# A hybrid recurrent and attention layer on one core: the second half of the program issued in stated order

## The chip, the cores and the metric

The kernel runs on one core of a Trainium2 chip. The core has a matrix engine (PE, with its weight loads shown apart as PEld), a vector engine (DVE), a scalar engine (ACT), GpSimd (POOL) and a sync engine (SP). In this kernel SP and POOL issue all DMA transfers; POOL issues nearly all stores of the second half, SP nearly all loads. The metric is the device time of one execution in microseconds, the median of several runs.

## The reference

The reference is one inference step of one layer, for a prompt of 2048 frames and a running stream of 64 frames, all in float32:

```python
xn = rmsnorm(x, norm_mix)
x_rnn, y_gate, q, k, v, g_rnn, g_attn = split(xn @ w_in)          # 1024 -> 5632
xc = causal_dwconv(x_rnn, width 4);  h = rg_lru(xc)               # linear recurrence
y_rnn  = h * gelu(y_gate)
y_attn = banded attention of 16 heads over 4 key groups, with rotary q, k and a sink logit
mixed  = sigmoid(g_rnn) * y_rnn + sigmoid(g_attn) * y_attn
x = x + mixed @ w_out                                              # 1024 -> 1024
up = rmsnorm(x, norm_ffn) @ w_up                                   # 1024 -> 5632
gate, val = split(causal_dwconv(up, width 3))
x = x + (silu(gate) * val) @ w_down                                # 2816 -> 1024
y = rmsnorm(x, norm_final)
```

Besides `y` it returns the new attention caches, the recurrent state and the convolution states.

## The kernel before

The frames of both streams stand side by side, 2112 columns, with channels on the 128 partitions. Every float32 product is made of three products in a reduced float32 format: an operand is split into a high part (`hi`, an ACT copy, line 198) and a low part (`lo = src - hi`, mostly on DVE, line 199), and `hi*hi`, `hi*lo` and `lo*hi` are added up in PSUM. So each operand that reaches PE has passed ACT and then DVE.

**First half.** Input projection, recurrence and attention, in three column blocks, up to `es1.close()` at line 719. The last thing that it leaves behind is the tensor `mixS` in DRAM.

**Output projection** (`wout`, `residual`, `mixes`, `wload`, `wsplit`, the loop from line 1258). The columns are taken in three pairs of blocks: phase 0 and phase 1 with two blocks of 304 columns, phase 2 with two of 448. In each phase a loop over `m` (8 row tiles of the output) calls `rows` (POOL loads of `x`), `wout` (48 matmuls over two half tiles of weights `j = 2m, 2m + 1`), `residual` (DVE adds, POOL stores to `x1S`, squares on ACT) and `drive(side, ...)`, which runs some steps of a side job. In phase 0 the weights come raw from DRAM (`wload`, line 375, two buffers), are split (`wsplit`) and their halves are stored to `woS` for the later phases, which load them from there (line 378). The side job of phase 0 is `mixes(1)` and `mixes(2)`: it loads `mixS` for the two later phases (line 358) and splits it, five steps behind each `m`. It has two buffers from line 1262 on, and the text of one step is a split followed by the load that takes over the buffer just split:

```python
        for j, (k, t0, n) in enumerate(todo):
            split(xblocks[t0][:, k, 0], xblocks[t0][:, k, 1], raw[j])
            load()
            yield
```

The side job of phases 1 and 2 is `xprep` (lines 773 to 815): it loads `x1S`, normalizes it (DVE, line 788), forms sums and differences and splits them into operands of the up projection.

**Up projection** (loop from line 1316). It is a fast matrix product with seven products in place of eight for each 2 by 2 block, so a group of weight rows takes seven steps `u = 0..6`. In steps 0 to 139 of the plan two lanes (two pairs of column blocks) share a group's weights; steps 140 to 167 have one lane each; the last 77 have two lanes on the third pair. One step states, in this order: work put off from earlier steps (`later`, filled by `at(d, f)`: convolution, gate, sums, stores), the products on PE (lines 1038 to 1040, 12 matmuls a lane), `prepare(i + ahead)` (the weights of a later step: for four of the seven steps a sum or difference on DVE at line 905, then `hi`, then `lo`; in later groups a load of the stored halves at line 901), `after(u)` (ACT copies of PSUM at line 1085, DVE sums at lines 1089, 1091 and 1096, ACT convolution term at line 1068), and then background jobs: `drive(x1, 5)` in the first four steps, `drive(fill, 1)` from step 6 on (`xsums`, lines 951 to 986, and `wsums`, lines 919 to 949, which prepare operands of the third pair), `xread` in the steps with one lane and the first of the third pair.

**Down projection** (loop over `seq`, line 1444 on). The same fast product in seven parts over 11 tiles; the weights are drawn from DRAM and combined (`draws`), the tokens loaded from `hS` (line 1207) and split (`parts`), with the final residual (`resid`, line 1422), squares and norm as side jobs.

What sets the order: tile buffers in this half are parts of a few large regions, handed out in the order of the text. The framework follows which instruction needs which other through them, and it decides the order in which each engine and each DMA queue gets its instructions: it takes the earliest in the text that a timing model says is ready, so instructions whose inputs the model expects late are passed by others. The order is fixed when the program is built; on the chip each engine runs its list from the front, and an instruction waits on semaphores for what it needs.

Of the kernel before, what the change touches and what calls it, by code (L numbers as in the profile page):

```python
# [126 lines left out]
def kernel(ctx: ExitStack, tc: tile.TileContext, xT, w_in, w_out, w_up, w_dn, gw, pk,  # L127
# [591 lines left out]
    es1.close()  # L719


    es2 = ExitStack()
    pff = es2.enter_context(tc.tile_pool(name="pff", bufs=5, space=PSUM))
    bank = [0]

# [926 lines left out]
```

## Time and profile before

| what | value |
|---|---|
| median of 3 runs | 3017.7 us (3002.41, 3018.79, 3017.7) |
| the profiled execution's own time | 3009.77 us |
| its span (first to last instruction) | 3008.0 us |
| mean granted clock of PE | 0.982 |
| matmuls | 17640 |

The profile was taken of one execution. Its page gives busy times, shares and the costliest groups of instructions; views of the trace give the same for any stretch of the span, group instructions by line, list them in order of time, or sum who waited for whom. In the view of windows each row is a stretch in us from the span's start, then the busy time of each engine with its number of instructions, the granted PE clock (1.00 is full), the busy share of the DMA engines and what they moved. The output projection begins at about 1366 us, the up projection at 1582 us, the down projection at 2530 us. Matmuls overlap, so the distance between their starts, not their duration, says how fast they follow each other.

### The profile page before, as it was taken

The page shows a single profiled execution, that of the slowest core. Times are in us where ns is not written, and L with a number is a line of the kernel's source. Part 1 is how long each engine was busy: PE and PEld are TensorE (multiplying, and loading weights), DVE is VectorE, ACT ScalarE, POOL GpSimd, SP SyncE. Part 2 cuts the span into 40 slices and gives each one's busy share as a digit, 9 for nine tenths or more (in the row PEclk, how much of TensorE's full clock was granted, in tenths as well). Part 3 has the DMA queues.
Part 4 walks back from the last instruction along what each step waited for, and adds up shares of the span by engine and source line. Part 5 has one row for each costly group of instructions (what it writes and reads, how often), then busy time and mean ns, then how long its engine had stood idle before and what let it go on. Part 6 is the DMA issues. An engine that isn't in the chain of part 4 may idle for free.

```text
span 3008.0 us, 49081 instructions
## 1 busy us (share of the span) xinstructions
PE 2877.2 (96%) x17640; PEld 2763.7 (92%) x17640; DVE 2052.4 (68%) x4048; ACT 1557.2 (52%) x3426; POOL 449.1 (15%) x655
## 2 busy tenths in 40 slices
PE   8999999999999999998999999999899999899998
PEld 7989888999998999997898999999899999799998
DVE  5288784377775277775669888777666657566766
ACT  4577772466763367764325445554544445334442
POOL 3232112000000000002222333222111111000001
PEclk9999999999999999999999999999999999999999
DMA  6766547543335643438776666555876667976653
GB/s 238 272 223 202 177 147 239 188 138 125 122 123 173 198 139 127 130 104 302 257 249 221 240 213 219 195 193 199 282 237 214 218 225 220 279 216 197 204 149 123
DMA packets 324501, 595.38 MB, mean 198 GB/s; under 512 B 37168, under 2 KB 224544, under 8 KB 307360
## 3 DMA queue, kind: packets, MB, share of 16 engines
q1 hardware_dynamic: 285728, 461.45, 48.6%
q0 software_dynamic: 38528, 130.79, 11.7%
q8 instruction: 139, 2.28, 0.3%
q14 instruction: 106, 0.87, 0.1%
HBM read 400.99 MB, written 191.64 MB: 197 GB/s over the span
## 4 chain that ended last, share of the span: by engine, by line
PE 68%; DVE 11%; DMA 8%; issue 7%; ACT 3%; POOL 2%; SPq 1%; DVEq 0%; POOLq 0%; ACTq 0%
PE mm L224 9%; PE mm L225 9%; PE mm L223 8%; PE mf L1038 4%; PE mf L1040 4%; PE mf L1039 4%; PE mf L1469 3%; PE mf L1470 3%; PE mf L1468 3%; PE mm L1038 3%; PE mm L1040 2%; PE mm L1039 2%; DMA FW<-mixS 2%; PE mm L1469 1%; PE mm L1470 1%
## 5 line engine op out<-in xcount | busy, mean ns | idle before, releaser
L223 PE MATMUL mm<-xh,whl 128*128 128x320 f32 (+2 forms) x2112 | 690.8, 327 | 11.3 <-ACT xh L198 5.9
L224 PE MATMUL mm<-xl,whl 128*128 128x320 f32 (+2 forms) x2112 | 689.2, 326 | 6.5 <-DVE xl L199 3.7
L225 PE MATMUL mm<-xh,whl 128*128 128x320 f32 (+2 forms) x2112 | 686.6, 325 | 1.4 <-POOL whl L199 1.4
L198 ACT ACTIVATE RE<-FW 128x512 fp32r<-128x512 f32 (+2 forms) x540 | 295.3, 559 | 384.4 <-PE mm L1470 59.2
L223 PEld LDWEIGHTS mm<-xh,whl 128*128 128x128 f32 x2112 | 401.4, 190 | 19.4 <-ACT xh L198 9.1
L224 PEld LDWEIGHTS mm<-xl,whl 128*128 128x128 f32 x2112 | 401.8, 190 | 15.9 <-DVE xl L199 6.5
L225 PEld LDWEIGHTS mm<-xh,whl 128*128 128x128 f32 x2112 | 402.2, 190 | 2.3 <-POOL whl L199 1.7
L199 DVE TENSOR_TENSOR RE<-FW,RE 128x512 fp32r<-128x512 f32 (+2 forms) x540 | 316.3, 600 | 127.1 <-ACT RE L198 125.6
L1038 PE MATMUL mf<-RA,RE 128*128 128x304 f32 (+1 forms) x608 | 200.4, 330 | 0.5 <-DVE FA L1089 0.5
L1040 PE MATMUL mf<-RA,RE 128*128 128x304 f32 (+1 forms) x608 | 199.7, 328 | 0.0
L1039 PE MATMUL mf<-RA,RE 128*128 128x304 f32 (+1 forms) x608 | 199.4, 328 | 0.0
L1469 PE MATMUL mf<-RE 128*128 128x304 f32 (+2 forms) x616 | 197.3, 320 | 0.6 <-DVE RE L199 0.6
L1468 PE MATMUL mf<-RE 128*128 128x304 f32 (+2 forms) x616 | 196.8, 320 | 0.0
L1470 PE MATMUL mf<-RE 128*128 128x304 f32 (+2 forms) x616 | 196.2, 319 | 0.0
L1038 PE MATMUL mf<-RE 128*128 128x304 f32 (+1 forms) x488 | 160.6, 329 | 12.6 <-ACT FA L1085 6.3
L1074 DVE SCALAR_TENSOR_TENSOR FW<-FA,pkt,FW 128x608 f32<-128x608 f32 x176 | 147.6, 844 | 18.3 <-ACT FW L1068 18.0
L1040 PE MATMUL mf<-RE 128*128 128x304 f32 (+1 forms) x488 | 159.9, 328 | 0.2 <-DVE RE L199 0.2
L1039 PE MATMUL mf<-RE 128*128 128x304 f32 (+1 forms) x488 | 159.6, 327 | 0.0
L199 POOL TENSOR_TENSOR gl<-gr,gh 128x256 fp32r<-128x256 f32 x24 | 22.3, 929 | 786.4 <-ACT gh L198 786.4
L1038 PE MATMUL mm<-RE 128*128 128x304 f32 (+1 forms) x392 | 126.5, 323 | 10.8 <-ACT FA L1085 7.6
L496 ACT ACTIVATE pr<-S,nm 128x256 f32<-128x256 f32 (+1 forms) x272 | 122.7, 464 | 12.6 <-DVE nm L492 12.4
L1040 PE MATMUL mm<-RE 128*128 128x304 f32 (+1 forms) x392 | 126.7, 323 | 2.7 <-DVE RE L199 2.7
(339 smaller groups left out, 7253.9 us busy)
## 6 DMA issues: line engine op xcount, KB each, us to landing
whl<-wiS SPq DMA_DIRECT2D x88, 1024.0 KB, 5.1
RE<-wuS SPq DMA_DIRECT2D x104, 512.0 KB, 4.4
wiS<-whl SPq DMA_DIRECT2D x44, 1024.0 KB, 4.8
wuS<-RE POOLq DMA_DIRECT2D x80, 512.0 KB, 4.1
FW<-in_w_up_dram SPq DMA_DIRECT2D x158, 256.0 KB, 3.5
hS<-FA POOLq DMA_DIRECT2D x154, 152.0 KB, 4.0
FW<-hS SPq DMA_DIRECT2D x154, 152.0 KB, 3.3
wraw<-in_w_in_dram SPq DMA_DIRECT2D x44, 512.0 KB, 5.8
```

What stands on the lines that cost most here:

```text
L198: nc.scalar.activation(hi, src, AF.Copy)
L199: (lo_eng or nc.vector).tensor_tensor(lo, src, hi.bitcast(F32), op=ALU.subtract)
L223: nc.tensor.matmul(ps[:, :n], wh[:, c], xh[:, k, :n], start=first, stop=False)
L224: nc.tensor.matmul(ps[:, :n], wh[:, c], xl[:, k, :n], start=False, stop=False)
L225: nc.tensor.matmul(ps[:, :n], wl[:, c], xh[:, k, :n], start=False, stop=last)
L1038: nc.tensor.matmul(ps[:, :n], w[:, 0, c], x[:, k, 0], start=first, stop=False, **more)
L1039: nc.tensor.matmul(ps[:, :n], w[:, 0, c], x[:, k, 1], start=False, stop=False, **more)
L1040: nc.tensor.matmul(ps[:, :n], w[:, 1, c], x[:, k, 0], start=False, stop=last, **more)
L1074: nc.vector.scalar_tensor_tensor(uc, G[:, j:j + self.cols], col("fw", 44 * j + m), uc, op0=ALU.mult, op1=ALU.add)
L1468: nc.tensor.matmul(ps[m][:, cs], w[:, 0, c], t[:, 0], start=k == 0, stop=False)
L1469: nc.tensor.matmul(ps[m][:, cs], w[:, 0, c], t[:, 1], start=False, stop=False)
L1470: nc.tensor.matmul(ps[m][:, cs], w[:, 1, c], t[:, 0], start=False, stop=k == 10)
```

## The change

The second half of the kernel is put under a scope in which every engine and every DMA queue takes its instructions in the order in which the text states them. No instruction, buffer or shape is changed; only the order in which each engine's and each queue's list is written. The scope holds to the end of the program, as `es2` is closed by its last line.

```diff
@@ -719,7 +719,9 @@
     es1.close()
 
 
+
     es2 = ExitStack()
+    es2.enter_context(tc.manual_schedule())
     pff = es2.enter_context(tc.tile_pool(name="pff", bufs=5, space=PSUM))
     bank = [0]
```

## The prediction

> **What bounds the kernel now.** The page's busy times say that PE works in nearly the whole span of 3008.0 us, and the view of windows says where it does not.
>
> ```profile
> PE 2877.2 (96%) x17640; PEld 2763.7 (92%) x17640; DVE 2052.4 (68%) x4048; ACT 1557.2 (52%) x3426; POOL 449.1 (15%) x655
> ```
>
> ```profile
> 1366.00:1441.00 75.00, 63.61 (x389) 58.76 (x388) 37.90 (x81) 29.78 (x64) 27.42 (x46) 0.90 0.96 339
> 1441.00:1505.00 64.00, 59.33 (x394) 57.69 (x393) 41.98 (x90) 24.45 (x52) 14.96 (x28) 0.95 0.79 253
> 1505.00:1582.00 77.00, 77.00 (x380) 71.16 (x379) 51.04 (x103) 21.47 (x45) 20.14 (x37) 1.00 0.75 249
> 1582.00:1890.00 308.00, 287.39 (x1964) 282.73 (x1963) 260.63 (x481) 152.88 (x364) 108.00 (x198) 0.97 0.65 225
> 1890.00:2090.00 200.00, 199.36 (x1410) 199.36 (x1411) 156.98 (x260) 106.02 (x246) 47.87 (x89) 0.98 0.54 186
> 2090.00:2160.00 70.00, 56.97 (x351) 54.02 (x351) 46.39 (x79) 35.64 (x79) 10.19 (x19) 0.90 0.82 271
> 2160.00:2560.00 400.00, 400.00 (x2042) 372.65 (x2041) 255.00 (x380) 193.99 (x464) 45.67 (x85) 1.00 0.71 228
> 2560.00:2630.00 70.00, 58.79 (x349) 54.48 (x348) 39.28 (x71) 23.23 (x50) 4.86 (x9) 1.00 0.96 283
> ```
>
> These windows are cut by stage: phases 0, 1 and 2 of the output projection, the two-lane steps of the up projection with and without background jobs, the one-lane steps, the third pair, and the start of the down projection. In phase 2 and from 2160 to 2560 PE is busy all the time, so order can give nothing there. In the other rows PE is busy 63.61 of 75, 59.33 of 64, 287.39 of 308, 56.97 of 70 and 58.79 of 70 us: some 61 us of idle PE is all there is to win, and a little more in clock. The change cannot make a matmul shorter; it can only move these waits, or add some.
>
> **Phase 0 of the output projection: +33 us.** This is the part on which the forecast rests. The next three fences are from the DMA view of phase 0 (issues, KB each, median us to landing), the same of phases 1 and 2, and the lists of ACT, DVE and PE in order of time.
>
> ```profile
> FW<-in_w_out_dram SPq DMA_DIRECT2D x16, 256.0 KB, 4.8
> FW<-mixS SPq DMA_DIRECT2D x24, 152.0 KB, 5.0
> ```
>
> ```profile
> FW<-x1S SPq DMA_DIRECT2D x32, 152.0 KB, 3.7
> ...
> FW<-mixS SPq DMA_DIRECT2D x9, 224.0 KB, 2.6
> ```
>
> ```profile
> 1402.82 0.46 ACT L198 ACTIVATE RE<-FW 128x304 fp32r<-128x304 f32 x1 [3.38 <-DMA FW<-mixS]
> 1403.18 0.62 ACT L198 ACTIVATE RA<-FW 128x512 fp32r<-128x512 f32 x1
> 1405.90 0.46 ACT L198 ACTIVATE RE<-FW 128x304 fp32r<-128x304 f32 x1 [2.10 <-DMA FW<-mixS]
> ...
> 1409.60 0.46 ACT L198 ACTIVATE RE<-FW 128x304 fp32r<-128x304 f32 x1 [2.89 <-DMA FW<-mixS]
> ```
>
> ```profile
> 1395.48 0.69 DVE L199 TENSOR_TENSOR RA<-FW,RA 128x512 fp32r<-128x512 f32 x1 [1.42 <-ACT RA L198]
> 1396.09 0.47 DVE L857 TENSOR_TENSOR FW<-FW 128x304 f32<-128x304 f32 x1
> 1396.48 0.47 DVE L199 TENSOR_TENSOR RE<-FW,RE 128x304 fp32r<-128x304 f32 x1
> ```
>
> ```profile
> 1386.34 0.30 PE L838 MATMUL mf<-RA 128*128 128x304 f32 x1
> 1386.47 0.30 PE L839 MATMUL mf<-RA 128*128 128x304 f32 x1
> ```
>
> Before, ACT alternates freely: a weight split (RA<-FW) goes in between single splits of `mixes` (RE<-FW), which come about 3 us apart, each waiting for its load. The weights for the next `m` do not wait for the five `mixes` steps of this one. Phases 1 and 2 still issue 9 of its loads. In the text all 32 splits are due by the end of phase 0, five behind each `m`, and nothing may pass them.
>
> One `m` in stated order, with L for a landing: the load of half tile 2m+3 is stated behind the split of 2m+2, and on SP behind the last `mixS` load of the former `m`, so it is issued only now, and its split on ACT ends L + 0.9 later (issue 0.3, split 0.6). Then its `lo` (0.69), the two DVE adds of the residual and the squares on ACT (0.4 each), 1.9 as a chain. Then two `mixes` splits whose loads have landed (ACT 0.46, DVE 0.47, 1 us), two whose buffers are free only behind them (L + 1), and the fifth the same way (L + 1). Together 5.8 + 3L per `m`, against 48 matmuls at 0.14 = 6.7 us on PE. `m` = 0 is done at 1382 us (its first DVE residual); its squares and four splits end at 1386 + L, five full rounds add 29 + 15L, and the last half tile with its matmuls 5 + L. So phase 0 ends at 1420 + 17L. In the present trace it ends at 1441.
>
> L was 5.0 where the DMA engines are 0.96 busy, 3.7 and 2.6 at about 0.77. The stage would move its 25 MB (339 GB/s x 75 us) in some 100 us, so the engines are busy about 0.7: I take 3.2, between the two rows at 0.77. 1420 + 54 = 1474, **+33**. Ends: L = 5.0 gives +64; the least landing of the `mixS` loads (line 358) bounds it from below:
>
> ```profile
> DMA to landing us min/median/max: 2.3/4.0/7.3
> ```
>
> 2.3 gives +18.
>
> **Phase 1: +4.** `xprep` loads stand on SP ahead of the `woS` loads for three `m` later, and each waits for a DVE or ACT step before it. With four scalings, seven splits and four sums at 0.39 to 0.45 us apart, and one exposed load landing per turn, DVE needs some 10.6 us an `m` while it lasts, PE 6.7. Three `m` of lead take up most of that; I reckon 68 us against 64: +4, between -5 (the idle PE of the window) and +15.
>
> **Two-lane steps of the up projection: +12.** The rows are from the groups by line, DVE and then ACT, without (1890 to 2090) and with background jobs (DVE, 1582 to 1960).
>
> ```profile
> L1074 DVE SCALAR_TENSOR_TENSOR FW<-FA,pkt,FW 128x608 f32<-128x608 f32 x69 | 58.3, 845 | 14.7 <-ACT FW L1068 14.7
> L199 DVE TENSOR_TENSOR RE<-FW,RE 128x512 fp32r<-128x512 f32 x57 | 39.1, 685 | 1.1 <-ACT RE L198 0.8
> L905 DVE TENSOR_TENSOR FW<-FW 128x512 f32<-128x512 f32 x32 | 21.9, 685 | 0.4
> ```
>
> ```profile
> L198 ACT ACTIVATE RE<-FW 128x512 fp32r<-128x512 f32 x58 | 36.2, 625 | 14.2 <-PE mf L1039 7.4 <-PE mm L1039 6.8
> ```
>
> ```profile
> L971 DVE SCALAR_TENSOR_TENSOR FA<-FA,pkt 128x224 f32<-128x224 f32 x32 | 13.6, 445 | 13.1 <-DMA FA<-x1S 13.1
> L199 DVE TENSOR_TENSOR RE<-FA,RE 128x256 fp32r<-128x256 f32 (+1 forms) x28 | 11.6, 439 | 5.8 <-ACT RE L198 5.8
> L978 DVE TENSOR_TENSOR FA<-FA 128x224 f32<-128x224 f32 x8 | 3.1, 386 | 0.1
> ...
> L947 DVE TENSOR_TENSOR FA<-FA 128x256 f32<-128x256 f32 x4 | 1.7, 421 | 0.1
> ```
>
> What goes: 1964 matmuls at 0.139 are 273 us, so 35 of 308 us are lost there now. About 10 of them belong to the entry at 1582, where `xprep` waits for its own loads in either order. The other 25 are in the stretch where the background jobs (L971 and its kin) run; in the text they are spread, one step each, up to step 111, and cannot push ahead of the copies and sums on which PE waits.
>
> What comes: line 905, the `hi` on ACT and the `lo` on DVE stand next to each other. Before, DVE does other work while ACT makes `hi` (0.8 us of waiting in all). In stated order DVE stands still each time, 0.63 + 0.1 us for the hand-over, x32 = 23 us in 200. DVE comes to (157 + 23) / 200 = 0.90. The background is 13.6 + 11.6, and four lines each like L978 and L947, 4 x 3.1 + 4 x 1.7: 44 us, over 105 steps of 3.34 us 0.13: 1.03, DVE becomes the bound. The wait of L1074 for L1068 (14.7 in 200, 0.07) follows from DVE's own line 1091 and stays: 1.10 x 351 us, 37 lost. 37 - 25 = **+12**. Ends: -25 if `hi` never delays DVE, and +31 if the waits of DVE for PE stay as well.
>
> **One-lane steps: -7.** The lists of DVE and PE in order of time, and a window behind the wait.
>
> ```profile
> 2103.91 0.48 DVE L1130 TENSOR_TENSOR FA<-FA 128x304 f32<-128x304 f32 x1 [5.95 <-DMA hS<-FA]
> 2104.30 0.47 DVE L1091 TENSOR_TENSOR FA<-mf,FA 128x304 f32<-128x304 f32 x1
> ```
>
> ```profile
> 2104.83 0.62 PE L1038 MATMUL mf<-RD,RE 128*128 128x304 f32 x1 [5.36 <-DVE FA L1091]
> ```
>
> ```profile
> 2104.00:2108.00 4.00, 3.17 (x12) 3.18 (x13) 2.86 (x5) 0.99 (x2) 0.54 (x1) 0.50 0.62 250
> ```
>
> A sum put off by five steps (line 1130) waits 5.95 us for a store, and the sum at line 1091, which the text has earlier, stands behind it. In stated order it goes first: 5.36 us, and the 12 matmuls behind it at 3.17 / 12 = 0.26 instead of 0.14 (granted clock 0.50), 1.4: -7. The rest of that stage's loss, 70 - 351 x 0.139 = 21 us, lies at a DMA share of 0.82 and at `xread`, two splits a step of 1.7 us; I leave it. Ends -13 and +8.
>
> The Trainium skill, page "PSUM — Partial Sum Buffer", section "Engine vs sequencer instructions", says that the queues of ScalarE, VectorE and GpSimdE are strict FIFO. By that rule the change is real, and it cuts both ways: each wait at the head of a list is paid by all behind it. This trace agrees in the 5.95 us above. Were it not so, both orders would run alike, at 3010.
>
> **Start of the down projection: -3.** Weights drawn and combined there come late; PE waits for the splits of tokens:
>
> ```profile
> PE mm L1469 <- DVE RE L199: 10.6, 8, 2.5
> ```
>
> The DMA engines are 0.96 busy there, so order can only bring the needed loads forward: -3, between -11 and +5. After 2630 nothing changes.
>
> **The sum.** 33 + 4 + 12 - 7 - 3 = +39. The profiled execution took 3009.77, with 1.8 us outside its span, and gives **3049**. It lay 8 us below the median of the runs, 3017.7; the forecast keeps to the profiled execution. A difference of 0.5% is about what a measurement of this kernel can tell from no change: faster is below 3003, slower above 3033.
>
> **The rivals.**
>
> *The background is the cost (faster).* In the up projection PE's waits come from work taken early; price 25 + 7 + 3 = 35. For: the 25 us lie just where the background runs, and the 5.95 us. Against: DVE at 1.03 and more. It decides if DVE keeps below PE's pace, and phases 0 and 1 together lengthen by less than 35, L below 3.0. At L = 2.4, 20 + 4 - 35 = -11: **2999**.
>
> *It cancels.* L = 2.6 (+23), half of the new 37 us on DVE: 23 + 4 - 7 - 7 - 3 = +10, **3020**.
>
> *Queues block all through.* L stays at 5.0, all DVE waits stay, `xread` blocks: 64 + 4 + 31 + 8 = 107, **3117**.
>
> *Nothing changes.* If the present lists were already those of the text: 3010. The trace speaks against it (1091 behind 1130).
>
> **How the numbers follow.** The forecast (3033 to 3075 by its own terms) gets 0.42, blocking throughout 0.10: slower 0.52. The background rival gets 0.30: faster. Cancelling 0.16 and nothing 0.02: same 0.18. For eight in ten the range runs from 2974, where all terms stand at their favourable ends (18 - 5 - 25 - 13 - 11 = -36), to 3105, which leaves out the worst of the blocking case.
>
> **What would show it.** Right: phase 0 ends near 1470, ACT there waits for `mixS` and `w_out` in turn and PE for `wsplit`; in steps 6 to 111 DVE's L199 waits for ACT L198 at some 0.7 us, over 30 us in all; no 5 us wait at 2100. Wrong: phase 0 ends by 1450, or PE runs without gaps from 1620 to 2090. What would overturn it most is a landing time in phase 0 well below 3 us.

## The result and the profile after

| what | before | after |
|---|---|---|
| median of four runs | 3013.2 us | 3155.02 us |
| the profiled execution's span | 3008.0 us | 3152.5 us |
| mean granted clock of PE | 0.982 | 0.965 |

The ratio is 1.0483, with a 95% interval of 1.0443 to 1.0523: the kernel is 142 us slower. The forecast was +39 us, and 3155 lies above its range. The first line of the changed kernel's page:

```profile
PE 2909.8 (92%) x17640; PEld 2788.1 (88%) x17640; DVE 2073.0 (66%) x4048; ACT 1547.2 (49%) x3426; POOL 449.8 (14%) x655
```

Each engine has as many instructions as before; its busy time moved little (DVE 2052.4 us before, ACT 1557.2). PE's idle time (span less busy time) grew from 131 to 243 us; the other 33 us are matmuls that took longer, at a lower clock. The stages in us, each cut from its first matmul to the first of the next, the last one at the end of the last matmul:

| stage | before | after | change | forecast |
|---|---|---|---|---|
| first half | 1367.1 | 1366.2 | -0.9 | 0 |
| output projection, phase 0 | 70.0 | 109.5 | +39.5 | +33 |
| phase 1 | 63.1 | 75.1 | +12.0 | +4 |
| phase 2 | 78.9 | 81.5 | +2.6 | 0 |
| up projection, steps 0 to 6 | 34.0 | 53.9 | +19.9 | } +12 |
| steps 7 to 139 | 472.6 | 508.1 | +35.5 | } |
| one-lane steps | 67.0 | 65.7 | -1.3 | -7 |
| third pair | 374.5 | 387.7 | +13.2 | 0 |
| down projection, matmuls 1 to 600 | 105.1 | 105.2 | +0.1 | -3 |
| down projection, the middle | 320.8 | 320.8 | 0 | 0 |
| the last 300 matmuls | 42.8 | 66.7 | +23.9 | 0 |

They add up to 144.5, which is the difference of the spans. The 0.1 of the first 600 matmuls of the down projection hides two larger changes: the first 300 took 56.3 us instead of 44.7, the next 300 as much less. The view of windows of the changed kernel, cut by these stages (the columns are those of the prediction: PE, PEld, DVE, ACT and POOL busy, then granted clock, DMA share, GB/s):

```profile
1370.00:1479.00 109.00, 74.51 (x382) 70.09 (x383) 41.71 (x84) 33.19 (x71) 28.82 (x48) 0.74 0.68 223
1479.00:1554.00 75.00, 60.82 (x390) 59.89 (x389) 44.14 (x95) 21.69 (x49) 17.47 (x32) 0.89 0.70 229
...
1636.00:1690.00 54.00, 30.90 (x175) 29.10 (x174) 36.67 (x63) 16.11 (x36) 4.86 (x9) 0.75 0.45 149
1690.00:2093.00 403.00, 368.90 (x2519) 361.22 (x2519) 316.12 (x550) 189.86 (x449) 125.83 (x231) 0.97 0.56 196
2093.00:2198.00 105.00, 97.44 (x677) 95.73 (x676) 80.28 (x133) 51.36 (x122) 24.91 (x46) 0.98 0.50 173
...
2651.00:2757.00 106.00, 97.43 (x603) 93.37 (x604) 62.38 (x113) 39.49 (x86) 9.71 (x18) 0.96 0.81 239
...
3077.00:3144.00 67.00, 44.84 (x313) 41.87 (x311) 41.78 (x83) 17.99 (x44) 12.35 (x23) 0.85 0.33 106
```

In phase 0 the DMA share fell to 0.68 from 0.96, in steps 7 to 111 to 0.56 from 0.62, and every engine is idle for part of the time there. The lists wait for each other. The places follow. Behind the change, line numbers of the changed kernel are two higher than before. A line of a sum of waits names who waited, for whom, the us in total, the number of times and the longest; a line in order of time has start, duration, engine, line and operation, and in brackets how long the engine stood idle before it and what ended that.

**Phase 0.** From the sums of waits and the list of DMA issues (KB each, median us to landing) of 1370 to 1479:

```profile
PE mf L840 <- ACT RA L198: 29.6, 6, 7.5
...
ACT RA L198 <- DMA FW<-in_w_out_dram: 27.6, 6, 6.0
...
ACT RE L198 <- DMA FW<-mixS: 24.0, 9, 4.1
```

```profile
FW<-in_w_out_dram SPq DMA_DIRECT2D x14, 256.0 KB, 4.4
FW<-mixS SPq DMA_DIRECT2D x15, 224.0 KB, 2.6
FW<-mixS SPq DMA_DIRECT2D x20, 152.0 KB, 2.3
```

ACT waits in turn for a weight load and for `mixS` loads, and PE for the `hi` of the weights. In the kernel before, PE's longest wait of this kind in phase 0 was 3.8 us (sums of waits of 1366 to 1441):

```profile
PE mm L838 <- ACT RA L198: 4.7, 3, 3.8
```

**Entry of the up projection.** ACT, DVE and PE in order of time, all around one matmul:

```profile
1654.15 0.63 ACT L198 ACTIVATE RE<-FW 128x512 fp32r<-128x512 f32 x1 [5.52 <-DVE FW L907]
1654.69 0.41 ACT L1087 ACTIVATE FA<-mf 128x304 f32<-128x304 f32 x1
1654.99 0.42 ACT L1087 ACTIVATE FA<-mm 128x304 f32<-128x304 f32 x1
```

```profile
1651.65 1.87 DVE L790 SCALAR_TENSOR_TENSOR FA<-FA,pkt,FW 128x304 f32<-128x304 f32 x4 [2.51 <-DMA FA<-x1S]
1653.44 0.68 DVE L907 TENSOR_TENSOR FW<-FW 128x512 f32<-128x512 f32 x1
```

```profile
1655.15 0.62 PE L1040 MATMUL mf<-RA,RE 128*128 128x304 f32 x1 [7.39 <-ACT FA L1087]
```

Read from the bottom up: PE waits 7.39 us for the copies that empty its accumulators (L1087). They stand in ACT's list behind a `hi` of weights (L198), which waits 5.52 us for the sum L907 on DVE, which stands behind four scalings (L790), which wait for a load. A weight of three steps later holds up the matmul that is due now. The rule quoted in the prediction, from the Trainium skill, page "PSUM — Partial Sum Buffer", section "Engine vs sequencer instructions" (strict FIFO lists), is what these rows show: the copies had nothing else to wait for.

**Steps 7 to 139.** The same pattern with smaller waits; the sums over 1690 to 2198:

```profile
ACT RE L198 <- DVE FW L907: 88.9, 40, 4.4
DVE RE L199 <- ACT RE L198: 75.3, 105, 1.9
...
PE mf L1040 <- ACT FA L1087: 21.3, 22, 2.6
...
PE mm L1040 <- ACT FA L1087: 17.0, 9, 4.3
```

In the kernel before, PE waited 13.6 us for these copies, DVE 6.6 us for `hi`, and `hi` for the sum 1.1 us (sums of 1617 to 2089):

```profile
PE mm L1038 <- ACT FA L1085: 7.6, 4, 2.9
...
DVE RE L199 <- ACT RE L198: 6.6, 7, 2.5
```

One such wait, from DVE, ACT and PE in order of time:

```profile
1750.58 1.49 DVE L1114 TENSOR_TENSOR FA<-FA,FW 128x608 f32<-128x608 f32 x2
```

```profile
1752.70 0.63 ACT L198 ACTIVATE RE<-FW 128x512 fp32r<-128x512 f32 x1 [2.56 <-DVE FW L907]
```

```profile
1753.70 0.41 PE L1040 MATMUL mf<-RA,RE 128*128 128x304 f32 x1 [1.86 <-ACT FA L1087]
```

Here DVE had not stood still: it was busy without a gap from 1745.94 on, with the gate (L1114) last, and the sum L907 came only behind that. ACT stood at `hi` meanwhile, with the copies behind it.

**Join to the down projection.** SP, ACT and PE in order of time:

```profile
2642.57 2.29 SPq L1209 DMA_DIRECT2D FW<-hS  x5
2644.97 1.52 SPq L1182 DMA_DIRECT2D FW<-in_w_dn_dram  x3
```

```profile
2649.46 0.63 ACT L198 ACTIVATE RE<-FW 128x512 fp32r<-128x512 f32 x1 [2.96 <-DMA FW<-in_w_dn_dram]
```

```profile
2651.34 0.62 PE L1470 MATMUL mf<-RE 128*128 128x304 f32 x1 [9.18 <-ACT RE L198]
```

The weight loads of the last step stand on SP behind token loads, which SP could issue only at 2642, after 13.2 us of waiting for a sum of the third pair on DVE (L1098); and the first tokens' splits stand on ACT behind the splits of those weights.

**Tail.** PE in order of time:

```profile
3099.41 1.86 PE L737 MATMUL mm<-FD,ones 128*128 128x448 f32 x2 [6.96 <-DVE FD L1439]
3112.00 1.38 PE L737 MATMUL mf<-FD,ones 128*128 128x304 f32 x2 [10.73 <-DVE FD L1439]
```

The text empties the whole list of norms 33 blocks ahead of the end. Its row sums are matmuls, so they stand in PE's list ahead of the last products, and PE stands for 17.7 us while DVE adds up the squares (L1439). Before, the framework's own order (called the planner's from here on) set the same two row sums 15 and 20 us into this stretch, with no wait (PE in order of time, the kernel before):

```profile
2971.54 0.91 PE L735 MATMUL mm<-FD,ones 128*128 128x448 f32 x2
2976.56 0.77 PE L735 MATMUL mf<-FD,ones 128*128 128x304 f32 x2
```

### The profile page after: what moved, and what is told of

Read it like the earlier page. It is cut to its first block, busy times and chain, and to the rows that moved or that the text cites. A ratio compares the mean times of both kernels' runs of the same rounds, so it can differ in the third digit from the quotient of the medians.

```text
span 3152.5 us, 48907 instructions
## 1 busy us (share of the span) xinstructions
PE 2909.8 (92%) x17640; PEld 2788.1 (88%) x17640; DVE 2073.0 (66%) x4048; ACT 1547.2 (49%) x3426; POOL 449.8 (14%) x655
## 5 line engine op out<-in xcount | busy, mean ns | idle before, releaser
L198 ACT ACTIVATE RE<-FW 128x512 fp32r<-128x512 f32 (+2 forms) x540 | 290.1, 558 | 491.0 <-DVE FW L907 97.0
L199 DVE TENSOR_TENSOR RE<-FW,RE 128x512 fp32r<-128x512 f32 (+2 forms) x540 | 315.7, 602 | 210.8 <-ACT RE L198 209.0
L1041 PE MATMUL mf<-RA,RE 128*128 128x304 f32 (+1 forms) x608 | 199.5, 328 | 0.0
L1041 PE MATMUL mf<-RE 128*128 128x304 f32 (+1 forms) x488 | 159.7, 327 | 0.0
L1040 PEld LDWEIGHTS mf<-RA,RE 128*128 128x128 f32 x608 | 116.2, 191 | 48.1 <-ACT FA L1087 40.2
L199 POOL TENSOR_TENSOR gl<-gr,gh 128x256 fp32r<-128x256 f32 x24 | 22.3, 930 | 788.7 <-ACT gh L198 788.7
```

Source lines behind the costliest of these rows:

```text
L198: nc.scalar.activation(hi, src, AF.Copy)
L199: (lo_eng or nc.vector).tensor_tensor(lo, src, hi.bitcast(F32), op=ALU.subtract)
L1040: nc.tensor.matmul(ps[:, :n], w[:, 0, c], x[:, k, 0], start=first, stop=False, **more)
L1041: nc.tensor.matmul(ps[:, :n], w[:, 0, c], x[:, k, 1], start=False, stop=False, **more)
```

## The experiments

All stages of all runs, cut as above, from the profiled execution of each (us). Where a run leaves both text and order of a stage as they were in the kernel before, its rows still differ by up to 5 us, so a difference of that size in one row says little:

| run | ph. 0 | ph. 1 | ph. 2 | steps 0-6 | 7-139 | one lane | third | down 600 | middle | last 300 |
|---|---|---|---|---|---|---|---|---|---|---|
| before | 70.0 | 63.1 | 78.9 | 34.0 | 472.6 | 67.0 | 374.5 | 105.1 | 320.8 | 42.8 |
| after | 109.5 | 75.1 | 81.5 | 53.9 | 508.1 | 65.7 | 387.7 | 105.2 | 320.8 | 66.7 |
| e1 | 109.0 | 73.8 | 81.2 | 35.6 | 469.8 | 67.5 | 376.4 | 103.4 | 320.8 | 42.8 |
| e2 | 70.8 | 66.2 | 80.8 | 51.2 | 507.5 | 63.2 | 399.0 | 104.4 | 320.3 | 43.1 |
| e3 | 70.2 | 63.3 | 78.9 | 34.5 | 469.3 | 66.6 | 375.6 | 108.8 | 320.3 | 65.2 |
| e4 | 94.9 | 68.9 | 78.9 | 32.4 | 466.1 | 61.8 | 378.5 | 106.0 | 320.3 | 42.8 |
| e5 | 101.4 | 74.7 | 81.5 | 54.5 | 508.6 | 64.4 | 398.1 | 104.5 | 320.8 | 65.3 |
| e6 | 109.5 | 73.2 | 83.6 | 51.4 | 531.7 | 69.1 | 395.5 | 108.0 | 320.3 | 61.0 |
| e7 | 107.4 | 77.1 | 81.2 | 53.4 | 462.0 | 64.4 | 389.5 | 105.8 | 320.3 | 65.2 |
| e8 | 69.8 | 62.7 | 78.9 | 34.0 | 467.4 | 65.7 | 383.3 | 103.4 | 320.3 | 42.8 |
| e9 | 108.7 | 75.4 | 81.6 | 51.1 | 507.3 | 64.4 | 389.9 | 104.2 | 327.4 | 43.2 |
| e10 | 68.8 | 62.8 | 79.9 | 36.0 | 472.0 | 67.5 | 375.7 | 105.6 | 320.3 | 42.8 |
| e11 | 68.0 | 66.0 | 78.9 | 35.3 | 463.1 | 62.9 | 376.6 | 104.5 | 320.8 | 43.1 |
| e12 | 69.7 | 81.4 | 84.9 | 46.0 | 462.0 | 67.6 | 390.9 | 104.3 | 328.2 | 43.2 |
| e13 | 82.7 | 80.9 | 83.8 | 53.4 | 509.8 | 63.9 | 386.1 | 110.0 | 320.8 | 66.3 |
| e14 | 72.5 | 61.3 | 79.3 | 35.1 | 459.9 | 65.3 | 377.0 | 105.0 | 320.8 | 42.8 |
| e15 | 109.2 | 74.9 | 83.5 | 51.3 | 493.2 | 62.7 | 396.2 | 105.8 | 327.9 | 43.2 |

### Which stage, and which lists (e1 to e4)

e1 holds the stated order for the output projection alone, e2 for the up projection alone, e3 for the down projection alone. The edit of e1 to the kernel before (in e2 and e3 the two places lie elsewhere):

```diff
+    order = ExitStack()
+    order.enter_context(tc.manual_schedule())
...
+    order.close()
     RC.close()
     FA = Region(tc, "FA", 28672, F32)
```

> The stated order holds for the output projection alone, up to its last matmul; from the up projection on the planner's order holds again. Measured between the two profiles, the three phases of the output projection grew by 39.5, 12.0 and 2.6 us, and the entry of the up projection (its first 7 steps) by 20. Theory (each stage pays for itself): phases 0 to 2 grow by 54 us here too, the entry by under 5, and nothing behind it, so some 3064 us against 3010 in a profile. Rival (a late output projection also puts work off into the up projection, which then pays for it): the entry keeps 15 to 20 us more, and the whole comes to 3075 to 3085.

> The stated order holds from the up projection's start to its last step, and nowhere else. Theory (each stage pays for itself): the entry +20, steps 7 to 139 +35, the third pair with the join to the down projection +13, together +67, 3077 us. Rival (part of the 35 us comes from work that the late output projection left behind, or the join's 9 us from the down projection's own order): the steps 7 to 139 keep below +20, or the join's wait of 9 us is gone, and the whole comes to 3040 to 3060.

> The stated order holds for the down projection alone. Theory: the tail grows by 24 us, because TensorE's row sums for the norm stand in its list ahead of the last matmuls and wait for VectorE's sums; the first 300 matmuls of the down projection lose what they lost (+11), matmuls 300 to 600 gain 11, and the whole is +24, 3034 us. Rival (the start's gain needs the third pair in stated order too): the first 600 matmuls keep the time of the kernel before within 3 us, or lose, and the tail still costs 24. If the tail's 24 us came from late splits of tokens instead, then waits for L198 and not for the squares' sum show there.

Measured medians: 3064.3, 3085.42 and 3034.2 us, beside 3008.53 for the kernel before. Each stage pays for itself. In e1 the entry took 35.6 us and the steps behind it 469.8, so a late output projection costs nothing later, and its rival fell. In e2 steps 7 to 139 took 507.5 against 508.1. In e3 the last 300 matmuls took 65.2; its first 600 lost 3.7 us, so the loss of the first 300 (56.9 us) was not made up in full there, as the rival had it. e2 came out 8 us above the 3077 expected; its third pair took 399.0, 11 us more than in the changed kernel (see the last section).

e4 states the order on SP and POOL alone (edit to the kernel before):

```diff
+    es2.enter_context(tc.manual_schedule(engines={mybir.EngineType.SP, mybir.EngineType.Pool}))
```

> The stated order holds throughout, but only on the two engines that issue the DMAs (SyncE and GpSimd); TensorE, VectorE and ScalarE keep the planner's order. Theory (the cost sits at the heads of the compute engines' lists): phase 0 still pays some 20 to 25 of its 39 us, since the loads of weights stand behind those of the mixed blocks on SyncE, the steps 7 to 139 of the up projection pay under 10 of 35, the tail under 3 of 24: in all +25 to +40, 3035 to 3050 us. Rival (the order of the DMA issues is what delays everything): +100 and more, with waits for DMA ahead of the splits in every stage.

Measured 3036.99 us. Phase 0 paid 24.9 of its 39.5 us, so the larger part of it lies on the queues; the steps of the up projection and the tail paid nothing, so their loss comes from the lists of PE, DVE and ACT. Steps 7 to 139 even took 6.5 us less than before, which had not been expected.

### Phase 0 and the join (e5, e13)

e5 states each weight load half a tile earlier:

```diff
-    wnext, xres = [3], {}
+    wnext, xres = [4], {}
...
-            while wnext[0] < 48 and wnext[0] <= j + (4 if wnext[0] > 15 else 3):
+            while wnext[0] < 48 and wnext[0] <= j + 4:
...
     wsplit(1)
+    wload(3)
```

> The changed kernel, with the loads of half weight tiles in phase 0 of the output projection stated one half tile earlier (into the buffer that is free by then), so that a split finds its load landed. Theory (in each m one landing of a weight load of some 4.5 us stands in ScalarE's list, ahead of the splits of mixed blocks): six to seven such waits go, phase 0 falls from 109.5 to 78 to 85 us, nothing else moves by over 4 us, and the whole is 25 to 30 us less than the changed kernel's 3155. Rival (the time sits in the mixed blocks' own two buffers and the landing only moves there): phase 0 keeps above 100 us.

Measured 3155.87 us: the rival held. Phase 0 took 101.4, only 8 us less, and the third pair 10 us more (see the last section), so the whole stayed. The sums of waits of e5 in phase 0:

```profile
ACT RE L198 <- DMA FW<-mixS: 35.7, 11, 5.0
...
ACT RA L198 <- DMA FW<-in_w_out_dram: 3.3, 1, 3.3
```

The weights' waits fell from 27.6 to 3.3 us as meant, but those for `mixS` rose from 24.0 to 35.7: their loads are issued as buffers come free, and what was left out in front of them was time in which they landed.

e13 leaves the weight loads and thins out the mixed blocks; at the join it puts the tokens' splits ahead of the weights':

```diff
             xk.reserve("xk", BM, 2)
-            side += [mixes(1, xk), mixes(2, xk)]
+            xk2 = Pool(FW)
+            xk2.slots["xk"], xk2.turn["xk"] = sums[2].slots["rs"], 0
+            side += [mixes(1, xk), mixes(2, xk2)]
...
-            drive(side, 5 if i == 0 else 1 if m == 0 else 4)
+            drive(side, 3 if i == 0 else 1 if m == 0 else 4)
...
-            drive(side, 99)
             wh0.close()
...
+        if left == 0:
+            parts(0)
+            parts(1)
         if left < 4:
...
-        if left == 0:
-            parts(0)
-            parts(1)
```

> The changed kernel with two edits in stages that do not touch. Phase 0: three steps of the mixed blocks per m instead of five, those of the third pair with two buffers of their own and finished in phase 1; the weight loads stay where they were. Theory (the five splits with two buffers, each a landing behind the other, set the pace of phase 0; the weight loads only share it): phase 0 falls from 109.5 to 80 to 90 us, phase 1 grows by 4 to 8. Rival (only both edits together free it, since any single landing left in ScalarE's list takes the whole turn): it keeps above 95, as with the weight loads alone (101.4). Join to the down projection: the splits of the first two token blocks are stated ahead of the three weight draws of the last step. Theory: TensorE's wait of 9.2 us there falls to some 5, as the tokens' own landing behind the freed memory stays. Rival (the loads on SyncE are what is late, in whatever order the splits stand): over 8.

Measured 3139.99 us. Phase 0 fell to 82.7 and phase 1 grew to 80.9, so the mixed blocks are the larger part. PE's wait at the join fell from 9.18 to 4.22 us, so ACT's list held it, but the first 600 matmuls then took 110.0 instead of 105.2: the same weights were late a few matmuls later. That part won nothing.

### The up projection (e6, e7, e9, e15)

At this point two theories stood for steps 7 to 139. **A**: PE waits for the copies because they stand on ACT behind a `hi` that waits for its sum. **B**, the prediction's: DVE stands still at every `hi` and becomes the bound.

e6 states the copies ahead of the weights of the same step, and in the tail the norms at two steps per block from 33 blocks ahead of the end:

```diff
+        for lane in live:
+            lane.after(u)
         while made <= i + ahead:
             prepare(made)
             made += 1
-        for lane in live:
-            lane.after(u)
...
+        if j >= len(seq) - 33:
+            drive(side, 1)
         if j == len(seq) - 33:
-            drive(side, 99)
             nc.scalar.activation(warm, epst, AF.Sqrt)
```

> The changed kernel with two edits in stages that do not touch. Up projection: in each step the copies and sums that empty the accumulators are stated ahead of the splits of weights. Theory A (the copies stand on ScalarE behind a hi split that waits for a sum on VectorE, and TensorE waits for the copies): steps 7 to 139 fall from 508 us to 475 to 485 (473 in the kernel before). Theory B, that of the prediction (VectorE stands 0.73 us at every hi split and so becomes the bound): these steps keep within 8 us of 508, since VectorE's work and waits stay. Tail: the list of norms is no longer emptied in one go 33 blocks ahead of the end, but two steps per block; theory: the last 300 matmuls take 43 to 48 us instead of 66.7; rival (the tail waits for splits of tokens): over 60.

Measured 3185.15 us, and both expectations missed. Steps 7 to 139 went up to 531.7. PE's waits in them:

```profile
PE mf L1040 <- ACT RE L198: 19.7, 13, 3.7
PE mf L1040 <- ACT FA L1087: 18.6, 18, 2.7
```

The copies passed the `hi` of their own step, but that of the step before still stood in front of them, and now the weights came too late as well. The tail took 61.0: PE still waited 2.1 and 5.7 us at the row sums, because DVE scaled the outputs of one block (L1452) ahead of the squares of the next.

e7 instead states each sum one step earlier, right behind the `lo` that it follows on DVE:

```diff
-        yield parts(r["11"])
-        yield kept_s(0, lambda: comb("11", "11", "21", ALU.subtract))
+        t = parts(r["11"])
+        early("11", "11", "21", ALU.subtract)
+        yield t
+        t = kept_s(0, lambda: r["11"])
+        early("11", "22", "11", ALU.subtract)
+        yield t
...
```

> The changed kernel, with each sum of weights in the up projection stated one step earlier, right behind the split that it follows on VectorE, so that no hi split waits for it. Theories A and B both say that the loss of steps 7 to 139 shrinks: by B all of VectorE's waits for hi (75 us) go and the steps fall to about 475; by A they fall as far as the copies come early, to 475 to 490. With the run before: if this one gains and the copies' place gains nothing, B is right; if both gain, A. If neither gains, the loss has another cause, and the waits of TensorE for L1087 stay over 60 us.

Measured 3110.26 us. Steps 7 to 139 took 462.0: the whole loss of the change went, and 10.6 us of the planner's too. The sums of waits in these steps (the copy is L1095 here):

```profile
ACT RE L198 <- DVE FW L908: 53.7, 29, 6.2
...
DVE RE L199 <- ACT RE L198: 24.6, 31, 1.9
...
PE mm L1048 <- ACT FA L1095: 5.8, 4, 3.1
```

By the expectation's own rule this spoke for B, but both waits had shrunk, and e6 had only shown that its edit was no test of A. e9 and e15 take away DVE's side alone: each `lo` is stated later, so that DVE never meets a `hi` that is still running, while `hi` waits for its sum as before (theory C, which is A without the copies' place in the step). In e9 the `lo` stands in the next step, in e15 at the end of its own:

```diff
-            split(t[:, 0], t[:, 1], src)
+            nc.scalar.activation(t[:, 0], src, AF.Copy)
+            los.append(lambda: nc.vector.tensor_tensor(t[:, 1], src, t[:, 0].bitcast(F32), op=ALU.subtract))
...
     def prepare(i):
+        while los:
+            los.pop(0)()
...
+        while los:
+            los.pop(0)()
         left = len(plan) - 1 - i
```

Both also empty the list of norms from 77 blocks ahead of the end. The second of the two `while` loops is in e15 alone.

> The changed kernel; in the up projection each lo split on VectorE is stated one step later than its hi, so that VectorE never waits for hi, while hi on ScalarE still waits for its sum on VectorE as before. Theory B (VectorE's standing at hi is the cost): the waits of L199 for L198, 75 us, fall below 20, and steps 7 to 139 fall from 508 to 480 or less. Theory C (what counts is the other side: hi stands in ScalarE's list waiting for a sum behind VectorE's backlog, and all of ScalarE's work behind it, copies and splits, waits too): the waits of L199 go as well, those of L198 for the sum (89 us) stay over 60, and the steps keep above 495. Between 480 and 495: both. In the tail the list of norms is emptied at two steps per block from 77 blocks ahead of the end instead of 33; theory: the last 300 matmuls take 43 to 48 us, as no backlog of norms stands ahead of TensorE's row sums; rival: they stay near the 61 us of the run that began 33 blocks ahead.

> As the run with lo one step late, but each lo stands at the end of its own step, behind the sums and background jobs of that step. The run before this one answered with a cost of its own: TensorE's waits for the copies (L1087) fell from 38 to 14 us, and 20 us of waits for lo (the third matmul of a trio) took their place, so that the steps kept 507 us and neither theory fell. Here lo is some two steps ahead of its matmul. Theory B (VectorE's standing at hi carries the loss): waits of lo for hi under 20 us, waits for lo under 5, steps 7 to 139 at 480 or less. Theory C (hi's waiting in ScalarE's list for its sum carries it): waits of hi for the sum over 60, waits of TensorE for the copies over 25, steps above 495. Both sides carry it: 480 to 495, waits for the copies of 10 to 25.

Measured 3142.34 and 3128.35 us. In e9 the steps took 507.3, with a wait of its own that PE had not had (sums of waits, e9):

```profile
PE mf L1043 <- DVE RE L895: 12.0, 11, 1.8
...
PE mm L1043 <- DVE RE L895: 8.0, 7, 1.4
```

L1043 is the matmul that needs `lo`: now it was late by 20 us, so e9 decides nothing. e15 is clean of that. PE, ACT and DVE in the sums of waits of e15 (L1041 is the matmul that waits for the copies, L1088):

```profile
PE mf L1041 <- ACT FA L1088: 17.3, 17, 2.4
PE mm L1041 <- ACT FA L1088: 14.5, 8, 3.5
...
ACT RE L894 <- DVE FW L908: 78.1, 39, 3.6
...
DVE RE L895 <- ACT RE L894: 25.1, 39, 0.8
DVE RE L199 <- ACT RE L198: 17.9, 16, 3.4
```

L895 is the `lo` of weights, L199 here that of the background jobs. Together 43.0 us of DVE's waits for `hi` are left of 75.3, those of `hi` for the sum stayed at 78.1 of 88.9, and the steps took 493.2. That is 15 us of the 46 that e7 won; the other 31 went only when the sum was early. The expectation's signs are mixed: the steps lie where both sides carry the loss, the waits for the copies (31.8 us) and of `hi` for the sum where theory C has them. DVE's side has a part, as 15 us went with 43% of its waits. That ACT's side has one is shown by waits like the one at 1752.70, ahead of which DVE had worked for 6 us without standing at a `hi`, and by DVE in e15: it waited 34.6 us for PE's products (lines 1092 and 1094), 7.7 us in the changed kernel, and PE still waited 31.8 of 38.3 us for the copies. How much is ACT's stays open: at most two thirds, since e15 took away less than half of DVE's side, and by the totals alone it could be little. In both runs the last 300 matmuls took 43.2 as expected, but the 320.8 us ahead of them became 327.4 and 327.9: 17 of the tail's 24 us are won.

### All in one text, and versions against both (e8, e10, e11, e12, e14)

e12 keeps the stated order throughout and mends the text: the edits of e5 and e7, the mixed blocks as in e13 (with four buffers for the second pair's), the norms from 77 blocks ahead, and two buffers for each load at the entry:

```diff
+            if two:
+                x = dict(nxt)
+                load(k + 1, *where)
             for o, (half, t) in where.items():
                 nc.vector.scalar_tensor_tensor(x[o], x[o], col("g2", k + half), rs[t], op0=ALU.mult, op1=ALU.mult)
```

> The changed kernel with its text mended in four places, stated order throughout: weight loads one half tile earlier in phase 0, the mixed blocks of the third pair with buffers of their own and mostly in phase 1 (three steps per m instead of five), two buffers for each load at the entry of the up projection, sums of weights one step earlier, and the norms from 77 blocks ahead of the end. Theory (each loss is a place where a list's head waits, and goes with that place): phase 0 falls from 109.5 to 85 or less, the entry from 54 to 40 to 45, steps 7 to 139 to about 462, the last 300 matmuls to 43 to 48, in all some 3050 us. Rival for phase 0 (the residual's chain between VectorE and ScalarE sets its pace, not the landings): it keeps above 95.

Measured 3058.12 us. Phase 0 took 69.7, as before the change: the two loads together free it (8 and 27 us alone, 40 together), as either one keeps the turn if left. Phases 1 and 2 grew by 6.3 and 3.4 over the changed kernel for what was moved there. The entry took 46.0, 8 us of its 20; no run shows what the other 12 are made of. It lies 50 us above its own runs of the kernel before (3008.05), where the change had cost 142: some 92 us are undone by moving statements and buffers.

e10 has e7's early sums under the planner's order, with no scope at all:

> The kernel before, in the planner's order, with each sum of weights in the up projection stated one step earlier. If the planner had put the sums well already, nothing changes within 0.3% (3000 to 3010 us). If its own order keeps them late, steps 7 to 139 fall from 473 towards 462, and the whole to 2995.

3010.0 us, ratio 1.0002 (0.9991 to 1.0013): no change. The planner gained nothing from the early sums, so by the expectation it had set them well already.

e8 keeps the planner's order and states that of SP and POOL alone, from the up projection's start to the end of its second pair; e11 has the early sums and the stated order on all engines from step 7 to the end of the one-lane part; e14 is e11 with steps 112 to 139 left to the planner:

```diff
+        if i == 112:
+            order.close()
+        if i == 7 or i == 140:
+            order = ExitStack()
+            order.enter_context(tc.manual_schedule())
```

> The kernel before, with the stated order on SyncE and GpSimd alone, and only from the up projection's start to the end of its second pair. The run with queues in stated order throughout gained there (32.4 + 173.1 + 197.4 + 95.6 + 61.8 = 560.3 us against 573.6 before), as no load of the background jobs comes early. Theory: that gain of 10 to 14 us is the queues' own and the rest stays as before: 2996 to 3000 us in a profile. Rival (the gain came from work that the slow output projection had put off or done): under 4 us, 3006 to 3010.

> The kernel before with the sums stated one step earlier and the stated order on all engines from step 7 of the up projection to the last one-lane step; the planner's order before and behind it. Theory (the early sums remove the one cost of the stated order there, and the gain is that background jobs no longer run ahead): steps 7 to the end of the one-lane part take 526 us instead of 540, the rest is as before, and the whole is 12 to 15 us less, 2990 to 2996. Rival (the gain is given back in the third pair, as with the queues alone, which gained 10 and lost 9 there): 3000 to 3010.

> The kernel before with the early sums and the stated order in steps 7 to 111 and in the one-lane part, the planner's order in steps 112 to 139, where the run with the stated order from 7 to the end of the one-lane part took 98.3 us against 93.7 before. Theory (stages stay additive): steps 112 to 139 take 94 us, the others as in that run, 2 to 5 us less than its 3000.7, 2995 to 2999. Rival (work put off from step 111 comes due there, or the one-lane part loses its gain of 4 us): 3000 or more.

e8: 3006.2 us, ratio 0.9998 (0.9978 to 1.0018), no gain. Steps 7 to 139 gained 5 us, no more than rows differ by chance, and the third pair lost 9, most of it to the slower matmuls of the last section. **e11: 3000.7 us, ratio 0.997 (0.9957 to 0.9984)**, 0.3% under the kernel before, and the interval leaves out 1. Steps 7 to the end of the one-lane part took the 526 us expected (463.1 + 62.9), but the whole won 8 us instead of 12 to 15 and lies where the rival had it. The third pair gave back only 2 us; the rest is spread over stages that the run left alone, in steps no larger than chance. Its window of steps 7 to 111:

```profile
1621.00:1986.00 365.00, 355.98 (x2523) 353.35 (x2522) 317.50 (x555) 189.09 (x452) 125.83 (x231) 1.00 0.62 215
```

It holds 2523 matmuls in 365 us at a clock of 1.00; the kernel before took 378.9 us for these steps (7 to 111). DVE does the same work (317.50 us). e14: 3000.87 us, ratio 0.9972 (0.9957 to 0.9986). Its time, 3000 or more, is where its rival had it, and equals e11's. Steps 112 to 139 took 96.8 instead of the 94 expected and the one-lane part gave back 2.4, both within chance.

## Why the prediction was wrong

The direction held, and the part that carried the most weight came as foretold; the size missed by 105 us (144.5 less 39).

- **Phase 0, +33: right.** 39.5 measured. It ended at 1479, not 1474; the loads landed in 4.4 and 2.3 to 2.6 us, so three landings make 9.2 us per `m` where 3 x 3.2 = 9.6 were taken. ACT's 15 waits for landings shown above add up to 51.6 us, where 17 of 3.2 make 54. That one landing time for both kinds of loads gave the right sum was partly luck: one kind came well above 3.2 and the other well below. As a sum it was right; as three separable terms it was not, for e5 took one of them away and won 8 us instead of some 26.
- **Phase 1, +4; phase 2, nothing.** 12.0 and 2.6: the first inside its bound of +15, by the path named. PE waited 14.2 us for stored weights (4.4 before), whose loads stand on SP behind `xprep` loads (L784) that waited 31.9 us for DVE (L799; 12.9 before). "PE is busy all the time, so order can give nothing there" held for a gain and was silent on a loss.
- **Two-lane steps, +12: the step that failed.** Measured +55.4, nearly twice its upper end of +31: +19.9 at the entry, +24.5 in steps 7 to 111 (378.9 to 403.4), +11.0 in steps 112 to 139 (93.7 to 104.7). The wait of DVE for `hi` came as foretold (75.3 us in 105 waits, 0.72 each), and so did DVE's load: in steps 7 to 111 it was busy 316 us and stood 59.3 us at `hi`, 375 us where 1.03 x 351 = 362 were forecast (sums of waits of 1690 to 2093):

```profile
DVE RE L199 <- ACT RE L198: 59.3, 83, 1.9
```

The failing step is that the exchange DVE, ACT, DVE was priced on DVE alone, as what DVE has above PE's pace. So steps 112 to 139, with DVE at 0.90, got no term, and steps 7 to 111 too small a one. The price missed the other half: on ACT `hi` waits for a sum behind DVE's backlog, with the copies for which PE waits behind it (the rows at 1752.70; e7, e15). That costs PE time also where DVE has time to spare: in steps 112 to 139 DVE was busy or stood at `hi` for 96 of 104.7 us, and 11 us were lost. The entry, put at "10 in either order", is the same fault with a load's landing in it: +19.9.
- **The background's 25 us.** In part. In e7 and e11 these steps took 462.0 and 463.1, some 10 us under the planner's, with the same work, and the sums alone won nothing under the planner (e10). e14 took 459.9. So 10 to 13 us come from order; the rest of the 25 came back in no run.
- **One-lane steps, -7.** -1.3. The 5.4 us wait for L1091 is gone, as foretold, but PE now waits 8.2 us for stored weights in this part (0.8 before; sums of waits of the changed kernel):

```profile
PE mf L1040 <- DMA RE<-wuS: 4.8, 3, 3.1
PE mm L1040 <- DMA RE<-wuS: 3.4, 3, 2.7
```

- **Down projection, -3; "after 2630 nothing changes".** The start came to +0.1, as +11.6 in its first 300 matmuls and as much less in the next; the join ahead of it cost 9.18 us and the tail 23.9, for which the prediction had no term. A stretch where PE is busy without a gap was taken as safe, though the planner had moved row sums out of the way there.
- **The rivals.** "Queues block all through", 3117 at a chance of 0.10, was nearest in time. It looked for the time in landings of 5.0 us in phase 0, which were not there, and in the waits that B names.

Summed up: 43 of the missing us were in the two-lane steps, 13 in the third pair (9 of them at the join), 24 in the tail, 17 in the output projection, 6 in the one-lane part and 3 at the down projection's start, less 1 ahead of it all.

## What to carry to other kernels

Taking the choice of order away from a planner is a change at every place where the text has something in front that is not ready, also in stages that show no wait now: read the text there for what stands ahead of PE's next instruction on each list, and follow it across two engines, not one. Where a value goes from DVE to ACT and back, state the first half of the trip a step ahead of the second. And a stated order is worth its place only by stretch: here from step 7 to the one-lane part, with the sums early, it won 0.3% over the planner, and in every other stretch it lost or won no more than chance.

## What the runs showed of the hardware

The matmuls of 448 columns came in two speeds at the same granted clock. Windows of the third pair of the kernel before and of e8:

```profile
2250.00:2350.00 100.00, 100.00 (x495) 92.67 (x494) 61.38 (x88) 46.80 (x113) 11.28 (x21) 1.00 0.68 217
```

```profile
2250.00:2350.00 100.00, 100.00 (x486) 90.81 (x485) 59.22 (x86) 45.74 (x109) 11.27 (x21) 1.00 0.64 213
```

PE is busy throughout in both, yet 495 matmuls start in one and 486 in the other: 0.2027 and 0.2067 us from start to start. A speed was kept over hundreds of us; in e8 it changed at 2183 us, next to one step of 0.33 us from start to start, and stayed so to the end of the third pair. Over the 375 us of the third pair it makes some 7 us, in e2, e5, e6, e8 and e15, and so it hides gains of that size. What sets it is open.

A long wait of PE cost more than itself here. Behind the 9.18 us at the join:

```profile
2651.30:2656.00 4.70, 4.51 (x16) 4.18 (x17) 3.55 (x8) 2.38 (x7) 0.00 (x0) 0.50 0.54 157
2656.00:2661.00 5.00, 5.00 (x38) 5.00 (x37) 4.93 (x7) 2.52 (x4) 0.00 (x0) 0.99 0.25 70
```

For 4.7 us the granted clock is 0.50 and 16 matmuls start, where the next 5.0 us hold 38. In phase 0, with a wait in nearly every `m`, the clock is 0.74 on the mean.
